# Two expert stages rearranged: whole-row weight loads, a new pair order and a split scatter in the first; permuted channels and two unsplit blocks in the second

## The chip, the cores and the metric

The kernel runs on one core of a Trainium2 chip. The metric is the device time of one execution in microseconds. Three runs of the kernel before took 1739.23, 1738.76 and 1736.85 us, median 1738.76 us.

## The reference

512 tokens of 1024 channels pass through two transformer blocks, everything in and out in float32. What matters here are the two mixture-of-experts parts:

```python
def expert_choice(h, w_router, w_gate, w_up, w_down):      # first block: 16 experts, FF 1024
    cap = CAP_FACTOR * l // N_EXPERTS                       # 64 tokens for each expert
    aff = softmax(h @ w_router)
    vals, idx = lax.top_k(swapaxes(aff, 1, 2), cap)
    xs = h[bidx, idx]
    hid = silu(xs @ w_gate) * (xs @ w_up)
    y = (hid @ w_down) * vals[..., None]
    return zeros_like(h).at[bidx, idx].add(y)
...
x = x + ga2 * expert_choice(hx2, ...)
...
def hierarchical_moe(h, ...):                               # second block: 16 experts, FF 256, top 2
    ...
    u = silu(h @ w_gate[e]) * (h @ w_up[e]) * combine[e]
    y = sum over e of u @ w_down[e]
```

The first block before that is an ada-norm, an mLSTM and a Fourier branch over the sequence and a context; the second has a conformer convolution, a forgetting attention and a cross attention ahead of its experts. A row norm ends each.

## The kernel before, in words

One class, `Builder`, writes the program in phases, and a scheduler orders the instructions of each engine by their place in the program and by due times. All weights that pass through the core come through one ring of 1-MB buffers, `raw` tiles of 128 partitions x 2048 float32. `self.raw` (L118 in its helper) lets SyncE issue the load of the next buffer in program order; a load waits for the readers of what the buffer held before. More buffers join the ring as memory comes free (`extra_raw`).

**First expert stage** (`phase_b`, from L1049). The 16 experts go in 8 pairs. 64 tokens of each of the two experts stand side by side in a tile of 128. One pair of them takes 24 MB of weights, 192 MB for the stage: `w_gate`, `w_up`, `w_down` of 1024x1024 float32 for each expert. A chunk of one load, `chunk_b`, is 512 rows by half of the columns (128x4x512), so a row of a load has 2 KB. For a pair:
- `gather` (L1069, its products L1077) picks the tokens by products of the residual `xres` with a 0/1 matrix `G`, 32 of 128x128x128 in float32. It stands inside the pair before.
- `pair_mm` (L1058) multiplies one half of the columns: gate half 0, up half 0, silu and product, four transposes (L1110), then the same of half 1, then down half 0 and half 1. The two experts' products (L1065, L1066) run beside each other in the two halves of the array's columns.
- After each down half, VectorE writes `y` = result times the gate vector `ga2` (L1117), TensorE multiplies it by a float32 matrix `PT` that holds the router's values at the tokens' places (L1120, 4 products), and VectorE adds the four tiles to the accumulator `acc` (L1122).

In the last pair the adds go to `xres`, from which the second block starts (L1222). Part of the first chunks are loaded ahead, in `phase_a2` (`keys`, `preload`).

**Second expert stage** (`phase_d`). For each expert up to 128 token rows are fetched from a memory copy of the normalised rows, `hmd`, which `write_rows` (L1643) fills; they are transposed (L1831) and split into a high and a low part in the reduced float format (`split`, L188 on ScalarE and L189 on VectorE). For each of 8 blocks of 128 channels the gate and up weights (128x512, `raw`) are split as well: `wH` on ScalarE (L129) and `wL` = raw - `wH` on VectorE (L130); three passes (L89, L90, L91) make one product. The weights are loaded in 1-KB rows. The down weights are split into `dH` (ScalarE) and `dL` (GpSimd, L1859), and the results are written to memory by an indirect transfer (L1883).

Of the kernel before, what the change touches and what calls it, by code (L numbers as in the profile page):

```python
# [8 lines left out]
F32 = mybir.dt.float32  # L9
F32R = mybir.dt.float32r  # L10
# [22 lines left out]
NRAW_B4 = 2  # L33
# [48 lines left out]
class Builder:  # L82
# [764 lines left out]
    def phase_a2(self, late, pb, right):  # L847
# [106 lines left out]
        keys = [(n, e, kk, h) for h in range(2) for n in ("w_gate_e", "w_up_e") for kk in (0, 4) for e in range(2)]  # L954
# [72 lines left out]
    def chunk_b(self, name, e, kk, half):  # L1027
        key = name, e, kk, half
# [15 lines left out]
    def phase_b(self, pb, right, G0):  # L1044
# [13 lines left out]
        def pair_mm(w, p, half, act):  # L1058
            ps = self.ps()
            for kk in (0, 4):  # L1060
                rA = chunk(w, 2 * p, kk, half)
                rB = chunk(w, 2 * p + 1, kk, half)
                for q in range(4):
                    k = kk + q
                    nc.tensor.matmul(ps[0:64, :], act[:, k, 0:64], rA[:, q, :], start=k == 0, stop=k == 7, tile_position=(0, 0))  # L1065
                    nc.tensor.matmul(ps[64:128, :], act[:, k, 64:128], rB[:, q, :], start=k == 0, stop=k == 7, tile_position=(0, 64))  # L1066
            return ps
# [16 lines left out]
        nxt = gather(0)  # L1084
        for p in range(8):
            xT = nxt
            if p == 0:
                nc.sync.dma_start(out=self.iota, in_=I["iota"])
                for e in range(2):
                    nc.sync.dma_start(out=ga2[:, e, :], in_=self.gad[1:2, e * 512:(e + 1) * 512].to_broadcast([128, 512]))  # L1090
            PT = xp.tile([128, 512], F32, tag="PT", name="PT", bufs=1)
            V.tensor_scalar(PT, self.iota, self.idxF[:, p:p + 1], self.valF[:, p:p + 1], op0=OP.is_equal, op1=OP.mult)
# [8 lines left out]
            hT = xp.tile([128, 8, 128], F32, tag="hidT", name="hidT", bufs=1)  # L1101
            for half in range(2):
                pg = pair_mm(w_g, p, half, xT)
                pu = pair_mm(w_u, p, half, xT)
# [7 lines left out]
                if half == 0 and p < 7:  # L1112
                    nxt = gather(p + 1)
# [925 lines left out]
```

## Time and profile before

| what | value |
|---|---|
| runs of the kernel before | 1736.85 to 1739.23 us, median 1738.76 us |
| the profiled execution: its own time | 1735.82 us |
| its span in the trace, granted clock over it | 1733.9 us, 0.975 |
| PE busy | 1580.3 us (91%) |
| PE weight loads | 1044.1 us (60%) |
| DVE, ACT, POOL busy | 881.7 (51%), 622.5 (36%), 536.7 (31%) us |
| moved by DMA | 381.22 MB, 220 GB/s on average |

The span is the time between the first and the last record of the profiled execution; 1.9 us of its own time lie around it. The shares are averages over stages that differ: the first expert stage takes the stretch from 544 to 1043 us, in which the DMA engines move about 386 GB/s, and the second expert stage the one from about 1520 to 1693 us, in which VectorE, ScalarE and TensorE are all busy. Both are read by windows, by the intervals between instructions that come once for each pair or expert, and by the waits.

### The profile page before, as it was taken

The numbers are of one execution on the slowest core, as the hardware profiler recorded it, in microseconds if no ns is written. First come the engines' busy times: TensorE is split into PE (matmuls) and PEld (weight loads), VectorE is DVE, ScalarE is ACT, GpSimd is POOL, SyncE is SP. The second block draws the span as 40 slices with busy tenths as digits, with TensorE's granted clock in tenths as the row PEclk, the third lists the DMA queues.
The fourth block names the chain that finished last, engine by engine and source line by source line (L and its number), as shares of the span: only waits on it lengthen the run. The fifth ranks groups of instructions, "written<-read, shape, count | busy, mean of one in ns | idle before, by whom it ended". The sixth has DMA issues, their size and how long they took to land. (4 is left out here: it accounts for less than half of the span.)

```text
span 1733.9 us, 20855 instructions
## 1 busy us (share of the span) xinstructions
PE 1580.3 (91%) x7734; PEld 1044.1 (60%) x7734; DVE 881.7 (51%) x1625; ACT 622.5 (36%) x1261; POOL 536.7 (31%) x433
## 2 busy tenths in 40 slices
PE   5988999999999999999999988999999988889984
PEld 3766677777776344344344326778666766666663
DVE  5388554433563212122122117998654464578886
ACT  3433354433432000000000015324763354478883
POOL 1213324334522000000000014575443342456654
PEclk9998999999999999999999998999999999899997
DMA  9533313445757999999999984323112329489934
GB/s 305 164 99 101 115 55 116 151 151 174 267 186 272 381 386 387 386 387 386 386 386 386 387 317 141 96 75 98 49 49 73 133 68 321 161 264 338 323 111 163
DMA packets 237227, 381.22 MB, mean 220 GB/s; under 512 B 16302, under 2 KB 107510, under 8 KB 237116
## 3 DMA queue, kind: packets, MB, share of 16 engines
q1 hardware_dynamic: 232796, 371.63, 61.2%
q0 software_dynamic: 4320, 8.16, 1.3%
q8 instruction: 63, 1.03, 0.3%
q14 instruction: 48, 0.39, 0.1%
HBM read 367.40 MB, written 19.93 MB: 223 GB/s over the span
## 5 line engine op out<-in xcount | busy, mean ns | idle before, releaser
L130 POOL TENSOR_TENSOR wL<-raw,wH 128x512 fp32r<-128x512 f32 x220 | 311.9, 1423 | 421.3 <-ACT wH L129 393.0
L129 ACT ACTIVATE wH<-raw 128x512 fp32r<-128x512 f32 x368 | 226.3, 629 | 283.8 <-PE ps L90 149.2
L1065 PE MATMUL ps<-raw,xT 128*64 128x512 f32 x512 | 228.5, 601 | 0.9 <-DMA raw<-in_w_up_e 0.9
L1066 PE MATMUL ps<-raw,xT 128*64 128x512 f32 x512 | 227.2, 601 | 1.6 <-DMA raw<-in_w_up_e 1.6
L1222 POOL TENSOR_TENSOR xg<-xres,raw 128x512 f32<-128x512 f32 x4 | 5.0, 1288 | 494.1 <-DVE xres L1122 494.1
L1066 PEld LDWEIGHTS ps<-raw,xT 128*64 128x64 f32 x512 | 69.3, 138 | 137.9 <-issue 132.2
L130 DVE TENSOR_TENSOR wL<-raw,wH 128x512 fp32r<-128x512 f32 x148 | 127.3, 906 | 27.0 <-ACT wH L129 25.5
L91 PE MATMUL ps<-raw,wL 128*128 128x512 f32 (+1 forms) x320 | 120.2, 376 | 2.9 <-POOL wL L130 2.9
L90 PE MATMUL ps<-raw,wH 128*128 128x512 f32 (+1 forms) x320 | 121.2, 379 | 0.0
L89 PE MATMUL ps<-raw,wH 128*128 128x512 f32 (+1 forms) x320 | 120.9, 379 | 0.0
L1107 DVE TENSOR_TENSOR hid<-hid,ps 128x512 f32<-128x512 f32 x16 | 11.0, 688 | 214.6 <-PE ps L1066 214.6
L1106 ACT ACTIVATE hid<-ps 128x512 f32<-128x512 f32 x16 | 9.6, 597 | 303.8 <-PE ps L1066 303.8
L1285 DVE SCALAR_TENSOR_TENSOR cacc<-upad,dwc,cacc 128x512 f32<-128x512 f32 x120 | 117.8, 1034 | 0.9
L1065 PE MATMUL ps<-raw,hidT 128*64 128x512 f32 x256 | 115.0, 596 | 0.0
L1066 PE MATMUL ps<-raw,hidT 128*64 128x512 f32 x256 | 113.5, 595 | 0.4 <-DMA raw<-in_w_down_e 0.4
L89 PE MATMUL ps<-hx,wH 128*128 128x512 f32 x224 | 91.7, 409 | 3.3 <-ACT wH L129 3.3
L91 PE MATMUL ps<-hx,wL 128*128 128x512 f32 x224 | 90.7, 405 | 2.2 <-POOL wL L130 2.0
L90 PE MATMUL ps<-hx,wH 128*128 128x512 f32 x224 | 90.4, 404 | 0.0
L1859 POOL TENSOR_TENSOR dL<-raw,dH 128x512 fp32r<-128x512 f32 x64 | 82.3, 1306 | 22.1 <-ACT dH L1858 21.6
L1066 PEld LDWEIGHTS ps<-raw,hidT 128*64 128x64 f32 x256 | 33.7, 137 | 72.1 <-issue 69.3
L1065 PEld LDWEIGHTS ps<-raw,xT 128*64 128x64 f32 x512 | 69.2, 138 | 11.0 <-issue 8.9
L1120 PE MATMUL pa<-y,PT 128*128 128x512 f32 x128 | 59.2, 605 | 12.3 <-DVE y L1117 12.3
(610 smaller groups left out, 3472.7 us busy)
## 6 DMA issues: line engine op xcount, KB each, us to landing
raw<-in_w_gate_e SPq DMA_DIRECT2D x64, 1024.0 KB
raw<-in_w_up_e SPq DMA_DIRECT2D x64, 1024.0 KB
raw<-in_w_down_e SPq DMA_DIRECT2D x64, 1024.0 KB
raw<-in_w_in SPq DMA_DIRECT2D x34, 1024.0 KB
raw<-in_w_ada SPq DMA_DIRECT2D x24, 1024.0 KB
raw<-in_expert_w_gate SPq DMA_DIRECT2D x32, 512.0 KB
raw<-in_expert_w_up SPq DMA_DIRECT2D x32, 512.0 KB
raw<-in_expert_w_down SPq DMA_DIRECT2D x16, 1024.0 KB
```

Of the source, the lines that this page charges most:

```text
L89: mm(ps, l[0], r[0], start=first, stop=False)
L90: mm(ps, l[0], r[1], start=False, stop=False)
L91: mm(ps, l[1], r[0], start=False, stop=last)
L129: i = self.nc.scalar.activation(out=H, in_=raw_ap, func=AF.Copy)
L130: j = (eng or self.lsub).tensor_tensor(out=L, in0=raw_ap, in1=H, op=OP.subtract)
L1065: nc.tensor.matmul(ps[0:64, :], act[:, k, 0:64], rA[:, q, :], start=k == 0, stop=k == 7, tile_position=(0, 0))
L1066: nc.tensor.matmul(ps[64:128, :], act[:, k, 64:128], rB[:, q, :], start=k == 0, stop=k == 7, tile_position=(0, 64))
L1106: AC.activation(out=hid, in_=pg, func=AF.Silu)
L1107: V.tensor_tensor(hid, hid, pu, op=OP.mult)
L1120: nc.tensor.matmul(ps, PT[:, t * 128:(t + 1) * 128], y, start=True, stop=True)
L1285: V.scalar_tensor_tensor(acc, src, c, acc, op0=OP.mult, op1=OP.add)
L1859: (nc.gpsimd, V)[DL[i]].tensor_tensor(out=L, in0=src, in1=H, op=OP.subtract)
```

## The change

In the first expert stage:
- A chunk is 256 whole rows (128x2x1024, rows of 4 KB in a load). A pair takes 8 chunks of gate, 8 of up, 8 of down, each a MB as before; only the last pair's down weights stay in half rows (`last_down`).
- `pair_mm` fills both halves of the columns at once, in two accumulators, so gate, up and down are each one run of 32 products.
- The gate products of pair p+1 are placed ahead of the down products of pair p.
- In the scatter the matrix is an exact 0/1 matrix in the reduced format, the router's value goes into `y` (L1122 of the new kernel), and `y` is split into `yH` (ScalarE) and `yL` (GpSimd, VectorE in the last pair). Two passes (`mm2`, L96 and L97) take the place of one float32 product.
- One extra raw buffer less (`NRAW_B4` 2 to 1): 16 buffers instead of 17.

In the second expert stage the rows of `hmd` are written with their channels permuted, so that a partition holds 8 channels that follow each other in the weights; a weight load of half an expert's gate or up is then one run of 4 KB for each partition. Blocks 3 and 7 of the 8 are multiplied in float32 from `raw` by an unsplit `xF`; six of eight are split as before.

```diff
-NRAW_B4 = 2
+NRAW_B4 = 1
...
-        return self.raw(self.I[name][0][e, kk * 128:(kk + 4) * 128, half * 512:(half + 1) * 512]
-                        .rearrange("(k p) c -> p k c", p=128), 4, 512)
+        return self.raw(self.I[name][0][e, kk * 256:(kk + 1) * 256, :].rearrange("(k p) c -> p k c", p=128), 2, 1024)
...
+        def pair_mm(w, p, act):
+            pss = [self.ps() for _ in range(2)]
+            for kk in range(4):
+                rs = [chunk(w, 2 * p + i, kk) for i in range(2)]
+                for q in range(2):
+                    k = 2 * kk + q
+                    for h, ps in enumerate(pss):
+                        for i, r in enumerate(rs):
+                            o = slice(64 * i, 64 * i + 64)
+                            nc.tensor.matmul(ps[o, :], act[:, k, o], r[:, q, h * 512:(h + 1) * 512], start=k == 0, stop=k == 7, tile_position=(0, 64 * i))
+            return pss
...
+        def scatter(p, py):
+            P = xp.tile([128, 512], F32R, tag="PT", name="PT", bufs=1)
+            V.tensor_scalar(P, self.iota, self.idxF[:, p:p + 1], None, op0=OP.is_equal)
+            for e in range(2):
+                y = xp.tile([128, 512], F32, tag="hid", name="y", bufs=3)
+                V.scalar_tensor_tensor(y, py[e], self.valF[:, p:p + 1], ga2[:, e, :], op0=OP.mult, op1=OP.mult)
+                H, L = (xp.tile([128, 512], F32R, tag="yS", name=x, bufs=3) for x in ("yH", "yL"))
+                AC.activation(out=H, in_=y, func=AF.Copy)
+                (nc.gpsimd if p < 7 else V).tensor_tensor(out=L, in0=y, in1=H, op=OP.subtract)
+                for t in range(4):
+                    ps = self.pa()
+                    self.mm2(ps, P[:, t * 128:(t + 1) * 128], (H, L), True, True)
...
+        pg = pair_mm(w_g, 0, xT)
         for p in range(8):
+            hid = silu(pg)
+            nxt = gather(p + 1) if p < 7 else None
+            hT = hidden(hid, pair_mm(w_u, p, xT))
...
+            else:
+                xT = nxt
+                pg = pair_mm(w_g, p + 1, xT)
+            scatter(p, pair_mm(w_d, p, hT) if p < 7 else last_down(hT))
...
-                    self.hm_last = nc.gpsimd.tensor_tensor(out=hs[e], in0=xres[:, t, c], in1=gm[:, c], op=OP.mult)
+                    x, g = (v.rearrange("p (q k) -> p k q", k=8)[:, 4 * e:4 * e + 4, :] for v in (xres[:, t, :], gm))
+                    self.hm_last = nc.gpsimd.tensor_tensor(out=hs[e].rearrange("p (k q) -> p k q", k=4), in0=x, in1=g, op=OP.mult)
...
-                r = self.raw_tile(4, 512)
+                r = self.raw_tile(2, 1024).rearrange("p i (k f) -> p i k f", k=4)
                 for i, w in enumerate((w_g, w_u)):
-                    nc.sync.dma_start(out=r[:, :, i * 256:(i + 1) * 256],
-                                      in_=w[e, kk * 128:(kk + 4) * 128, :].rearrange("(k p) f -> p k f", p=128))
+                    nc.sync.dma_start(out=r[:, i], in_=w[e].rearrange("(p k) f -> p k f", k=8)[:, kk:kk + 4, :])
...
+                nc.scalar.activation(out=xF[:, e2, :], in_=ps[:, 384:512], func=AF.Copy)
...
+                w, j = rs[k // 4][:, :, k % 4, :], 3 * (k // 4) + k % 4
+                if k % 4 == 3:
+                    nc.tensor.matmul(pgu, xF[:, k // 4, :], w, start=False, stop=k == 7)
+                    continue
```

On TensorE, in the first expert stage, this is a piece of one pair in the kernel before; `hid` transposed, then the row of tokens `bcI`, the gather and the scatter (`y`, `PT`) stand between products of single halves.

```order
L1110 MATMUL pa<-ident,hid 128x128 x4
L1038 MATMUL bcI<-ident,idxF 128x128
L1066 MATMUL ps<-raw,xT 64x512
L1065 MATMUL ps<-raw,xT 64x512
L1077 MATMUL pa<-G,xres 128x128 x32
...
L1066 MATMUL ps<-raw,hidT 64x512
L1065 MATMUL ps<-raw,xT 64x512
L1120 MATMUL pa<-y,PT 128x512 x4
L1066 MATMUL ps<-raw,xT 64x512
```

In the new kernel one pair reads on TensorE as follows, from the up products (`xT`, 6 and 25 of them, one more further up) over the gate products of the next pair (1 and 31) to its down products (`hidT`) and the scatter.

```order
L1068 MATMUL ps<-raw,xT 64x512 x6
L1079 MATMUL pa<-G,xres 128x128 x32
L1068 MATMUL ps<-raw,xT 64x512 x25
L1106 MATMUL pa<-ident,hid 128x128 x4
L1068 MATMUL ps<-raw,xT 64x512
L1106 MATMUL pa<-ident,hid 128x128 x4
L1068 MATMUL ps<-raw,xT 64x512 x31
L1068 MATMUL ps<-raw,hidT 64x512 x32
L96 MATMUL pa<-yH,PT 128x512 x3
L97 MATMUL pa<-yL,PT 128x512 x3
L96 MATMUL pa<-yH,PT 128x512
L97 MATMUL pa<-yL,PT 128x512
```

Both transposes now stand near the start of the next pair's gate products, and the scatter of both halves comes together behind the 32 down products, with a single product of the following up run between.

On SyncE's queue the loads of one pair stood like this before.

```order
L118 DMA raw<-in_w_down_e 128x4x512 x8
L118 DMA raw<-in_w_gate_e 128x4x512 x4
L118 DMA raw<-in_w_up_e 128x4x512 x4
L118 DMA raw<-in_w_gate_e 128x4x512 x4
L118 DMA raw<-in_w_up_e 128x4x512 x4
L118 DMA raw<-in_w_down_e 128x4x512 x8
```

In the new kernel they stand so, the last row being the last pair's down weights.

```order
L118 DMA raw<-in_w_gate_e 128x2x1024 x8
L118 DMA raw<-in_w_down_e 128x2x1024 x8
L118 DMA raw<-in_w_up_e 128x2x1024 x8
L118 DMA raw<-in_w_gate_e 128x2x1024 x8
...
L118 DMA raw<-in_w_down_e 128x4x512 x8
```

The number of loads is the same, 24 a pair; gate comes ahead of the previous pair's down, and the rows are twice as long.

On VectorE one expert of the second stage was this (a number behind a name tells the expert's tile apart).

```order
L1843 TENSOR_TENSOR hid_11205<-hid_11205,egu 128x256
L130 TENSOR_TENSOR wL<-raw,wH 128x512
L189 TENSOR_TENSOR xL_11209<-pa,xH_11208 128x512 x2
L1878 TENSOR_SCALAR y_11224<-py_11225,wslv 128x512
L189 TENSOR_TENSOR hidL<-pa,hidH 128x256
L130 TENSOR_TENSOR wL<-raw,wH 128x512 x7
```

It is now this.

```order
L1886 TENSOR_TENSOR hid_11176<-hid_11176,egu 128x256
L189 TENSOR_TENSOR xL_11180<-pa,xH_11179 128x384 x2
L1921 TENSOR_SCALAR y_11198<-py_11199,wslv 128x512
L189 TENSOR_TENSOR hidL<-pa,hidH 128x256
L1882 TENSOR_TENSOR wL<-raw,wH 128x512 x6
```

Two of the eight subtractions for the weights are gone, all six that are left stand in one run behind `hidL`, and the split of the rows is a quarter shorter.

## Rows read from the trace of the kernel before

**Rows 1.** Windows: PE, PEld, DVE, ACT, POOL busy (count); clock, DMA share, GB/s.

```profile
550.00:995.00 445.00, 420.23 (x2042) 178.84 (x2040) 89.74 (x175) 19.71 (x33) 0.00 (x0) 1.00 1.04 386
980.00:985.00 5.00, 5.00 (x22) 2.15 (x22) 0.00 (x0) 1.20 (x2) 0.00 (x0) 0.68 1.04 387
1000.00:1005.00 5.00, 5.00 (x26) 1.63 (x24) 0.00 (x0) 0.00 (x0) 0.00 (x0) 1.00 0.03 9
```

**Rows 2.** One line's TensorE products, 520 to 1060 us: min/median/max ns, first, last.

```profile
L1065 PE MATMUL ps<-raw,xT x512: 592/592/1061, 544.4 to 1016.0; 128*64 128x512 f32 x171
```

**Rows 3.** Timeline of DVE: start, duration, line, tiles, idle time before and its releaser.

```profile
662.97 0.69 DVE L1117 TENSOR_TENSOR y<-ps,ga 128x512 f32<-128x512 f32 x1 [6.32 <-PE ps L1065]
724.87 0.69 DVE L1117 TENSOR_TENSOR y<-ps,ga 128x512 f32<-128x512 f32 x1 [6.32 <-PE ps L1065]
1038.16 0.69 DVE L1117 TENSOR_TENSOR y<-ps,ga 128x512 f32<-128x512 f32 x1 [6.32 <-PE ps L1066]
```

**Rows 4.** Waits, 540 to 1040 us: total us, times, longest.

```profile
PE pa L1120 <- DVE y L1117: 12.3, 16, 0.8
PE ps L1066 <- DMA raw<-in_w_up_e: 1.6, 1, 1.6
```

**Rows 5.** Windows with transfers of other row lengths.

```profile
345.50:347.50 2.00, 2.00 (x18) 1.96 (x17) 0.95 (x2) 0.80 (x2) 1.04 (x1) 1.00 1.09 349
409.00:411.50 2.50, 2.50 (x12) 2.03 (x11) 0.00 (x1) 0.84 (x2) 1.30 (x2) 1.00 1.01 409
1697.00:1703.00 6.00, 5.47 (x22) 3.22 (x20) 3.69 (x5) 3.33 (x7) 6.00 (x5) 1.00 1.02 414
```

**Rows 6.** The loads in these windows, timeline of SyncE's queue.

```profile
342.18 0.37 SPq L118 DMA_DIRECT2D raw<-in_w_ada  x1
407.09 0.38 SPq L118 DMA_DIRECT2D raw<-in_mem  x1
1693.43 2.19 SPq L1919 DMA_DIRECT2D raw<-yd  x4
```

**Rows 7.** Timeline of PE in the first expert stage.

```profile
537.12 7.31 PE L1077 MATMUL pa<-G,xres 128*128 128x128 f32 x64
602.24 3.70 PE L1120 MATMUL pa<-y,PT 128*128 128x512 f32 x8 [0.78 <-DVE y L1117]
606.78 0.59 PE L1066 MATMUL ps<-raw,xT 128*64 128x512 f32 x1
607.21 0.59 PE L1066 MATMUL ps<-raw,xT 128*64 128x512 f32 x1
```

**Rows 8.** Timeline of PE, second expert stage.

```profile
1604.53 0.50 PE L90 MATMUL egu<-wL,xH 128*128 128x512 f32 x1 [1.14 <-DVE wL L130]
1615.67 0.50 PE L90 MATMUL egu<-wL,xH 128*128 128x512 f32 x1 [1.11 <-DVE wL L130]
1616.00 0.39 PE L91 MATMUL egu<-wH,xL 128*128 128x512 f32 x1
1616.23 0.40 PE L89 MATMUL egu<-wH,xH 128*128 128x512 f32 x1
```

**Rows 9.** Window of one expert, second expert stage.

```profile
1604.70:1615.80 11.10, 9.91 (x47) 7.57 (x48) 9.55 (x14) 9.10 (x17) 7.38 (x6) 1.00 0.92 303
```

**Rows 10.** A group, 1560 to 1694 us: count, busy us, mean ns, idle before.

```profile
L130 DVE TENSOR_TENSOR wL<-raw,wH 128x512 fp32r<-128x512 f32 x97 | 85.1, 933 | 1.1
```

**Rows 11.** Timelines of DVE and of POOL in one expert.

```profile
1611.67 6.35 DVE L130 TENSOR_TENSOR wL<-raw,wH 128x512 fp32r<-128x512 f32 x7
1607.14 0.69 DVE L130 TENSOR_TENSOR wL<-raw,wH 128x512 fp32r<-128x512 f32 x1
1613.76 1.29 POOL L1859 TENSOR_TENSOR dL<-raw,dH 128x512 fp32r<-128x512 f32 x1
```

**Rows 12.** Timeline of POOL ahead of the second expert stage.

```profile
1506.00 2.49 POOL L1643 TENSOR_TENSOR hm<-xres,raw 128x512 f32<-128x512 f32 x2
1516.57 1.24 POOL L1818 DMA_INDIRECT xsb<-hmd,trow  x1 [5.41 <-DVE s L1771]
```

More of the change, by code (lines that the diff above doesn't have):

```diff
@@ L953, in phase_a2 @@
         self.pre = {}
-        keys = [(n, e, kk, h) for h in range(2) for n in ("w_gate_e", "w_up_e") for kk in (0, 4) for e in range(2)]
+        keys = [(n, e, kk) for n in ("w_gate_e", "w_up_e") for kk in range(4) for e in range(2)]
         def preload(n):
@@ L1083, in phase_b, with last_down @@
             nc.sync.dma_start(out=rows2[8 * i:8 * i + 8], in_=n.rearrange("(k p) -> k p", p=128))
-        nxt = gather(0)
-        for p in range(8):
[L1086 to L1092, printed above, removed]
+        def last_down(act):
+            pss = [self.ps() for _ in range(2)]
+            for h, ps in enumerate(pss):
+                for kk in (0, 4):
+                    rs = [self.raw(I[w_d][0][14 + i, kk * 128:(kk + 4) * 128, h * 512:(h + 1) * 512].rearrange("(k p) c -> p k c", p=128), 4, 512)
+                          for i in range(2)]
+                    for k in range(kk, kk + 4):
+                        for i, r in enumerate(rs):
+                            o = slice(64 * i, 64 * i + 64)
+                            nc.tensor.matmul(ps[o, :], act[:, k, o], r[:, k - kk, :], start=k == 0, stop=k == 7, tile_position=(0, 64 * i))
+            return pss
@@ new lines, in hidden @@
+        def hidden(pg, pu):
+            hT = xp.tile([128, 8, 128], F32, tag="hidT", name="hidT", bufs=1)
+            for half in range(2):
+                V.tensor_tensor(pg[half], pg[half], pu[half], op=OP.mult)
+                ps = self.pa()
+                for q in range(4):
+                    nc.tensor.transpose(ps[:, q * 128:(q + 1) * 128], pg[half][:, q * 128:(q + 1) * 128], ident)
+                AC.activation(out=hT[:, 4 * half:4 * half + 4, :], in_=ps.rearrange("p (k s) -> p k s", k=4), func=AF.Copy)
+            return hT
@@ new lines, in silu @@
+        def silu(pg):
+            hid = [xp.tile([128, 512], F32, tag="hid", name="hid", bufs=3) for _ in range(2)]
+            for h in range(2):
+                AC.activation(out=hid[h], in_=pg[h], func=AF.Silu)
+            return hid
+        def scatter(p, py):
[8 more added lines that the diff above has]
+                for t in range(4):
+                    ps = self.pa()
+                    self.mm2(ps, P[:, t * 128:(t + 1) * 128], (H, L), True, True)
+                    c = slice(e * 512, (e + 1) * 512)
+                    V.tensor_tensor((acc if p < 7 else xres)[:, t, c], (acc if p else xres)[:, t, c], ps, op=OP.add)
@@ L1093, in phase_b @@
+        xT = gather(0)
+        nc.sync.dma_start(out=self.iota, in_=I["iota"])
+        for e in range(2):
+            nc.sync.dma_start(out=ga2[:, e, :], in_=self.gad[1:2, e * 512:(e + 1) * 512].to_broadcast([128, 512]))
+        pg = pair_mm(w_g, 0, xT)
+        for p in range(8):
+            hid = silu(pg)
+            nxt = gather(p + 1) if p < 7 else None
+            hT = hidden(hid, pair_mm(w_u, p, xT))
             if p == 7:
@@ L1823, in expert_in @@
         def expert_in(x):
[L1825 to L1826 removed]
+            xH = xp.tile([128, 6, 128], F32R, tag="xH", name="xH2", bufs=NXH)
+            xL = xp.tile([128, 6, 128], F32R, tag="xL", name="xL2", bufs=NXH)
+            xF = xp.tile([128, 2, 128], F32, tag="xF", name="xF2", bufs=NXH)
             for e2 in range(2):
```

53 lines of the change are left out of this document (11 added, 42 removed).

## The prediction

> **What bounds the kernel now.** I read the windows first, because the change touches two stages and the averages over the span mix them. In the first expert stage TensorE is busy 420 of 445 us while the DMA engines are fully busy at 386 GB/s [rows 1]: two limits lie close together, and the reader has to find out which ends last. The interval between two scatters of the same kind tells TensorE's pace: y at 662.97 and at 724.87, so 61.9 us for a pair [rows 3]. The transfers' pace follows from their size: a pair takes 24 loads of 1.0486 MB, 25.17 MB, and at 386 GB/s that is 65.2 us. So the transfers are slower by 3.3 us a pair, but TensorE began at 544.4 [rows 2] with a full ring of 17 buffers, and a lead of 17 loads (46 us) lasts almost to the end. The waits agree: TensorE waited 1.6 us for a weight, once, and 12.3 us for `y` [rows 4]. The stage is balanced: whoever shortens only one side gains next to nothing.
>
> In the second expert stage the window of one expert has TensorE at 9.91, VectorE at 9.55, ScalarE at 9.10 of 11.10 us and the transfers at 0.92 [rows 9]; an expert takes 11.14 us (1604.53 to 1615.67), and both rows show TensorE idle 1.1 us until VectorE's `wL` [rows 8]. VectorE is not full, but its seven subtractions behind `hidL` take 6.35 us in a row [rows 11], and TensorE is at their end.
>
> **First expert stage, TensorE.** The expert products stay: a product of one expert shows as two records 0.43 us apart, with the other expert's beside it [rows 7], so 48 steps a pair (gate, up, down, each 8 blocks by 2 halves) take 48 x 0.86 = 41.3 us, before and after. The gather stays: 7.2 us for the first one, from 537.12 to the first product at 544.4 [rows 2, 7]. The scatter changes. Before, twice a pair, eight records in 3.70 us and a wait for `y` [rows 7], near 4.7 with the pipeline's restart, so 9 to 10 us. After, 4 tiles by 2 halves by 2 passes: a reduced-format pass of the same width follows the one ahead by 0.23 us (1616.00 to 1616.23) [rows 8], 16 x 0.23 = 3.7 us. The wait comes on top: `y` 0.69 us, `yH` about as much, then `yL` on POOL 1.29 (as for `dL`) [rows 3, 11], of which the passes that need `yH` alone cover 0.7; some 2 us, and the second half waits for nothing. That makes 5.7. The saving is 3.3 to 4.5 us, and the transposes of the hidden values, now behind a gate product, may give 0.8 more. TensorE's pair comes to 61.9 - 5.4 at best and 61.9 - 3.3 at worst, 56.5 to 58.6. The new work on ScalarE and POOL is free: POOL did nothing in the stage and ScalarE 19.7 of 445 us [rows 1].
>
> **First expert stage, transfers.** What decides is whether 4-KB rows move faster than 2-KB rows. Before does not show it on these weights; the nearest rows are loads of the same kind. Rows of 1 KB (`w_ada`) gave 349 GB/s, the 2-KB rows here 386, rows of 4 KB 409 (`in_mem`) and 414 (`yd`), with all engines full each time [rows 1, 5, 6]. The ends are 386 (no gain) and 414. I take 409, the load from an input by the same queue. A load then lasts 2.564 us instead of 2.716.
>
> The Trainium skill ("DMA: Bandwidth & Descriptors", section "Why small descriptors are slow") has a fixed overhead of about 3 cycles a packet, beside a cycle for each 32 bytes; by that, 4-KB packets are 2.2% faster than 2-KB ones, 395 GB/s, the last y falls at 1020.8 and the stage gains 17 us. The rows go against so small an effect, 6% between 386 and 409, and the measurement decides. The same page's section "Where 436 GB/s comes from" lets the memory side bind at about 358 GB/s, by which row length could not matter at all; 386 over 445 us contradicts the figure.
>
> The ring has 16 buffers now. All are full when TensorE starts, the first pair of loads is used up by 547.8 and the transfers run again from about 549.7. 176 of 192 loads are left: 168 x 2.564 + 8 x 2.716 (the last down, still 2 KB) = 452.5 us, until 1002.2; the products on the last load take 3.4, and the last y stands at 1005.5 instead of 1038.2 [rows 3]: 32.7 us earlier. TensorE by itself would end at 544.4 + 8P - 11 (the first gather lies ahead, 7.2, and the last scatter behind, 3.8): for P = 56.5 at 985, for 58.6 at 1002. So the transfers end last up to P = 59.1, and the shorter scatter matters only because it keeps TensorE under this. Against the gain stands a hole like the one before, where the queue moved 9 GB/s from 1000 to 1005 [rows 1] because `gg` had taken a slot of the ring; with TensorE now the one who waits, buffers are free earlier, and I deduct 2.5 us (0 to 5). Gain 30 us; by the ends of the rate, 7 to 38. Removing the 17th buffer costs its lead of one load, 2.6 us, which is in this count. The new order (gate ahead of the previous down) leaves the number of loads alone and only shifts which one TensorE waits for.
>
> **Second expert stage.** Without its waits TensorE needs for an expert 24 passes x 0.23, eight transposes 0.8, twelve down passes 2.8, two transposes 0.1, restarts 0.2, about 9.4 us. Six passes go (-1.4), two float32 products of 0.86 come (+1.7), with two changes of format about 0.1: 9.85. VectorE loses two of eight subtractions (933 ns on average, 0.69 undisturbed) [rows 10, 11] and a quarter of `xL`: 9.55 - 1.5 = 8.1. ScalarE loses two `wH`, gains two small `xF`: 9.1 becomes 8.2. So TensorE becomes the limit if the subtractions come in time: the fifth of the run is wanted about 8.0 us after the last product of the expert before, and comes at about 7.5 (hidden values, `hidL`, then five by 0.65, one of them stretched beside POOL's subtraction, which ran at 1613.76 while VectorE's seven took 6.35 instead of 7 x 0.62 = 4.3 us) [rows 11]. A cover of 0.5 us is thin. If it holds, 11.14 - 9.85 = 1.29 an expert, and over 14 experts in steady state (16 less the first and last) 18; I take 16.4, since the traces of experts differ by some tenths. If it fails the period is 10.95 and the gain 2.5. Transfers need 3.15 MB an expert, 7.7 us at 409 beside 0.92 of 11.1 us so far with 1-KB and 4-KB rows mixed [rows 9]; faster rows make this smaller.
>
> The permuted write of `hmd` reads both operands with a step of 32 bytes on POOL. Before, two take 2.49 us [rows 12]; the trace has no such read. The ends are no change and twice the time, 5 us for the last two. POOL then waits 5.4 us for the routing before its first row fetch [rows 12], and the cover is spoilt only beyond about 4 us, where the fill of `xsb`, queued behind it, and the fetch come later; at nothing. The Trainium skill ("GPSIMD Engine Reference", "Performance pitfalls for Q7 kernels") gives +50% for such a step; by it the last two take 3.7 us, inside the cover.
>
> **Sum.** 1735.8 (the profiled execution's own time) - 30 - 16.4 = 1689.4. The median of the runs is 2.9 above that execution, so 1692 for the median.
>
> **Rivals.**
> 1. Row length does nothing: 386 stays. Last y 549.7 + 176 x 2.716 + 3.4 = 1031.2, gain 7; 1735.8 - 7 - 16.4 + 2.9 = 1715. For it: 386 is flat over the whole stage. Against: two 4-KB loads above 409 [rows 5]. 10%.
> 2. VectorE still ends last in the second stage, period 10.95: 1735.8 - 30 - 2.5 + 2.9 = 1706. For it: the thin cover, and the stretched subtractions [rows 10]. Against: two of eight are gone. 22%.
> 3. TensorE stays the limit in the first stage, because `y` to `yL` runs over three engines while nothing is left to cover it: P = 61 gives a last y at 1021.4, gain 16.8, total 1705. For it: the wait for `y` now stands behind both halves at once. Against: it would have to cost 7 us where I count 2. 12%.
> 4. Slower: TensorE, which now waits for weights in every pair, is granted its lower level. In this stage the clock was 1.00 except for stretches like 980 to 985, 0.68 between the two levels of 1.2 and 2.4 GHz, with TensorE busy throughout [rows 1]. If the clock averages c in the stage, a pair takes 56.5/c and the last y stands at 544.4 + 8 x 56.5/c - 11. The second stage's 16.4 us are used up at a last y of 1054.6, P = 65.2, c = 0.87; at 0.80 the time is 1735.8 + 60 - 16.4 + 2.9 = 1782. Against it: one short drop in 445 us. 4%.
>
> **How the numbers follow.** Forecast 50%, with a range of its own of 1684 to 1700 (rate 414 at the one end, TensorE near 58 or a gap at the other); rivals as given, 2% for what I don't see. 1692 is the likeliest. For eight in ten: below 1676 would need more than both gains at their best; above 1720 lies rival 4 and rivals 1 and 2 together. Runs spread by 0.14%, so 0.2% (3.5 us) is what can be told from no change. All but rival 4 are faster: 0.93 faster, 0.03 the same (several rivals at once), 0.04 slower.
>
> **What the new profile would show.** Right: 405 to 415 GB/s over the first expert stage; TensorE's waits there name the weights' transfers, not `y`; y's 61 to 62 us apart once the ring's lead is gone, 56 to 59 before; the last y near 1006; an expert of the second stage in 9.8 to 10.1 us, with hardly a wait for `wL`; `hm` longer and no later first fetch. Wrong: 386 to 395 GB/s (rivals 1); periods of 11 with waits for `wL` (2); waits for `yL` or `y` of 5 us a pair with the transfers idle in between (3); a clock below 0.9 over tens of us (4).

## The result and the profile after

The changed kernel takes 1712.94 us (median of four runs, 1708.35 to 1715.06), the kernel before 1738.99 us beside it. The ratio is 0.985 with a 95% interval of 0.982 to 0.987: 22 to 31 us faster, where 47 was forecast. The profiled execution took 1714.9 us, its span is 1713.1 us, the granted clock 0.969. The sign held, and the time lies between the 1676 and 1720 that were given for eight in ten, but outside the forecast's own range of 1684 to 1700; the size was a little over half. The time is nearest to that of rival 1 (1715), whose mechanism did not come: the rate below shows it. So the total alone would have pointed at the wrong cause.

The way to see where it went is to cut both traces at the same five marks and compare the lengths (all from the timelines of the two kernels: the first product of the first pair, the last `y`, the first residual add ahead of `hm`, the first fetch of expert rows, the last indirect store).

| stretch (us) | before | after | gain | forecast |
|---|---|---|---|---|
| start to the first product of pair 0 | 544.4 | 546.2 | -1.8 | 0 |
| first product to last `y` | 493.8 | 472.5 | 21.3 | 30 |
| last `y` to the residual add | 445.8 | 446.2 | -0.4 | 0 |
| residual add to the first fetch of rows | 32.6 | 39.3 | -6.7 | 0 |
| first fetch to the last store | 173.8 | 166.6 | 7.2 | 16.4 |
| last store to the end | 43.5 | 42.3 | 1.2 | 0 |

The rows add up to 20.8 us, the difference of the two profiled executions; that of the kernel before lies under all four of its runs, that of the changed kernel is one of its two longest, and the medians differ by 26. The start is left unexplained: in the experiments below it lies between 542.1 and 547.8 without an edit ahead of it. The two expert stages gave 29 us instead of 46, and 6.7 were lost between them. The rest of this section shows the lines for each; the lines of before that they answer to are named.

**First expert stage.** Windows, columns as in [rows 1]:

```profile
800.00:900.00 100.00, 97.78 (x473) 41.24 (x474) 16.27 (x35) 4.62 (x8) 2.56 (x2) 1.00 1.03 409
995.00:1000.00 5.00, 5.00 (x19) 2.92 (x19) 0.00 (x0) 1.19 (x2) 0.00 (x0) 0.50 0.62 230
1000.00:1010.00 10.00, 9.01 (x38) 2.83 (x36) 0.00 (x0) 0.00 (x0) 0.00 (x0) 0.97 0.64 222
```

The rate is 409 GB/s, the value taken, instead of 386; and near the end there is a hole, with 230 GB/s from 995 to 1000 and less behind. VectorE's timeline gives the pairs ([rows 3]; here both halves of a pair come together):

```profile
669.28 1.54 DVE L1122 SCALAR_TENSOR_TENSOR y<-ps,valF,ga 128x512 f32<-128x512 f32 x2 [28.29 <-PE ps L1068]
727.48 1.54 DVE L1122 SCALAR_TENSOR_TENSOR y<-ps,valF,ga 128x512 f32<-128x512 f32 x2 [28.30 <-PE ps L1068]
907.62 1.54 DVE L1122 SCALAR_TENSOR_TENSOR y<-ps,valF,ga 128x512 f32<-128x512 f32 x2 [31.50 <-PE ps L1068]
969.02 1.54 DVE L1122 SCALAR_TENSOR_TENSOR y<-ps,valF,ga 128x512 f32<-128x512 f32 x2 [31.53 <-PE ps L1068]
1018.76 0.75 DVE L1122 SCALAR_TENSOR_TENSOR y<-ps,valF,ga 128x512 f32<-128x512 f32 x1 [0.48 <-PE ps L1096]
```

A pair takes 58.2 us while the ring still has a lead (669.28 to 727.48) and 61.4 us when it is gone (907.62 to 969.02; 24 loads at 409 GB/s take 61.5): TensorE's pace first, the transfers' pace afterwards, both as forecast. But the last `y` comes 49.7 us after that of the pair before. On TensorE's timeline, in this last stretch:

```profile
961.00 4.48 PE L1068 MATMUL ps<-raw,hidT 128*64 128x512 f32 x16 [0.48 <-DMA raw<-in_w_down_e]
966.12 3.65 PE L1068 MATMUL ps<-raw,hidT 128*64 128x512 f32 x12 [0.64 <-DMA raw<-in_w_down_e]
970.48 0.97 PE L96 MATMUL pa<-yH,PT 128*128 128x512 f32 x3 [0.72 <-ACT yH L1124]
...
991.84 5.38 PE L1148 MATMUL pa<-rows,ident 16*128 16x128 f32 x32
997.15 9.68 PE L1096 MATMUL ps<-raw,hidT 128*64 128x512 f32 x34
1007.82 3.78 PE L1096 MATMUL ps<-raw,hidT 128*64 128x512 f32 x16 [0.99 <-DMA raw<-in_w_down_e]
```

Until 968 TensorE waits for weights; after that only once, for 0.99 us, at the load that came out of the hole. Scatter, 32 up products, `gg` (L1148) and 32 down products are TensorE's own work, and a piece of it ran at the lower of the clock's two levels (0.50 from 995 to 1000, from the small products of `gg` on). SyncE's queue shows the hole itself, a load waiting from about 988 to 1002.6:

```profile
985.98 2.56 SPq L118 DMA_DIRECT2D raw<-in_w_down_e  x1
1002.57 1.47 SPq L118 DMA_DIRECT2D raw<-in_w_down_e  x3
```

**Between the stages.** POOL and VectorE, timelines ([rows 12] has the same stretch of before):

```profile
1470.96 4.07 POOL L1675 TENSOR_TENSOR hm<-xres,raw 128x512 f32<-128x512 f32 x2 [1.93 <-DVE xres L1217]
1474.98 0.55 POOL L235 TENSOR_TENSOR rr<-rv,mhalf 128x1 f32<-128x1 f32 x1
1490.80 4.07 POOL L1675 TENSOR_TENSOR hm<-xres,raw 128x512 f32<-128x512 f32 x2
1504.22 1.24 POOL L1850 DMA_INDIRECT xsb<-hmd,trow  x1 [6.68 <-DVE s L1791]
```

```profile
1477.54 2.00 DVE L230 TENSOR_TENSOR rv<-ss 128x1 f32<-128x1 f32 x1 [1.74 <-ACT nsq L1226]
```

Two `hm` take 4.07 us instead of 2.49. The last two are hidden, as forecast: POOL still idles 6.68 us before the first fetch. But `rr`, which the routing needs, stands behind the first ones in POOL's queue, and VectorE's tiny `rv` is longer beside them: the first two of the four take 1.36 and 2.00 us, in the kernel before 0.59 and 0.25.

**Second expert stage.** One expert's window, and ScalarE and TensorE in it ([rows 8, 9]):

```profile
1579.57:1590.20 10.63, 9.99 (x45) 7.32 (x44) 8.22 (x12) 8.02 (x18) 7.73 (x7) 1.00 0.94 361
```

```profile
1578.89 0.93 ACT L188 ACTIVATE xH<-pa 128x384 fp32r<-128x384 f32 x2
1581.50 0.28 ACT L1867 ACTIVATE xF<-pa 128x128 f32<-128x128 f32 x1 [1.68 <-DVE xL L189]
1581.67 0.62 ACT L1901 ACTIVATE dH<-raw 128x512 fp32r<-128x512 f32 x1
1584.48 0.39 ACT L188 ACTIVATE hidH<-pa 128x256 fp32r<-128x256 f32 x1
```

```profile
1576.14 0.50 PE L90 MATMUL egu<-wL,xH 128*128 128x512 f32 x1 [0.62 <-DVE wL L1882]
1586.77 0.50 PE L90 MATMUL egu<-wL,xH 128*128 128x512 f32 x1 [0.64 <-DVE wL L1882]
```

An expert takes 10.63 us. VectorE and ScalarE have nearly the busy times that the prediction gave them (8.22 and 8.02 against 8.1 and 8.2), yet TensorE still waits for `wL`. What is new is ScalarE's 1.68 us in front of `xF`: it idles until VectorE has made `xL` out of the same PSUM tile `pa`, into which TensorE transposed the rows. `dH` and `hidH` are queued behind `xF`, and VectorE's `hidL` and run of `wL` wait for `hidH`, so all of them start later.

### The profile page after: what moved, and what is told of

Read it like the earlier page. It is cut to its first block, busy times and chain, and to the rows that moved or that the text cites. A ratio compares the mean times of both kernels' runs of the same rounds, so it can differ in the third digit from the quotient of the medians.

```text
span 1713.1 us, 20867 instructions
## 1 busy us (share of the span) xinstructions
PE 1579.9 (92%) x7702; PEld 1049.7 (61%) x7702; DVE 856.2 (50%) x1595; ACT 613.5 (36%) x1277; POOL 564.9 (33%) x447
## 5 line engine op out<-in xcount | busy, mean ns | idle before, releaser
L129 ACT ACTIVATE wH<-raw 128x512 fp32r<-128x512 f32 x240 | 149.6, 628 | 256.8 <-PE ps L90 149.7
L1068 PE MATMUL ps<-raw,xT 128*64 128x512 f32 x1024 | 240.8, 595 | 0.0
L1068 PEld LDWEIGHTS ps<-raw,xT 128*64 128x64 f32 x1024 | 74.3, 137 | 137.3 <-issue 133.4
L1125 POOL TENSOR_TENSOR yL<-y,yH 128x512 fp32r<-128x512 f32 x14 | 17.9, 1278 | 419.4 <-ACT yH L1124 409.2
L1122 DVE SCALAR_TENSOR_TENSOR y<-ps,valF,ga 128x512 f32<-128x512 f32 x16 | 12.0, 751 | 228.0 <-PE ps L1068 206.8
L1068 PE MATMUL ps<-raw,hidT 128*64 128x512 f32 x448 | 109.3, 594 | 2.8 <-DMA raw<-in_w_down_e 2.8
L1882 DVE TENSOR_TENSOR wL<-raw,wH 128x512 fp32r<-128x512 f32 x96 | 88.4, 976 | 4.6 <-ACT wH L1881 3.3
L1124 ACT ACTIVATE yH<-y 128x512 fp32r<-128x512 f32 x16 | 10.0, 626 | 212.7 <-DVE y L1122 212.7
L91 PEld LDWEIGHTS ps<-raw,wL 128*128 128x128 f32 x320 | 61.2, 191 | 15.0 <-POOL wL L130 3.4
L89 PEld LDWEIGHTS ps<-raw,wH 128*128 128x128 f32 x320 | 61.4, 192 | 12.2 <-ACT raw L188 1.1
L90 PEld LDWEIGHTS ps<-raw,wH 128*128 128x128 f32 x320 | 61.1, 191 | 11.4 <-issue 0.5
```

The costliest lines, as they stand in the source:

```text
L89: mm(ps, l[0], r[0], start=first, stop=False)
L90: mm(ps, l[0], r[1], start=False, stop=False)
L91: mm(ps, l[1], r[0], start=False, stop=last)
L129: i = self.nc.scalar.activation(out=H, in_=raw_ap, func=AF.Copy)
L1068: nc.tensor.matmul(ps[o, :], act[:, k, o], r[:, q, h * 512:(h + 1) * 512], start=k == 0, stop=k == 7, tile_position=(0, 64 * i))
L1125: (nc.gpsimd if p < 7 else V).tensor_tensor(out=L, in0=y, in1=H, op=OP.subtract)
```

## The experiments

Three theories, one for each loss. **First stage:** the ring loses a buffer to `gg` and stalls, and TensorE's own work ends last. **Between:** `hm` with a step delays `rr` and `rv`. **Second stage:** `xF` behind `xL`. Each has a rival in its expectation. The stretches quoted are those of the table above, from one profiled execution each; where an edit doesn't touch them they lie from 470.5 to 472.5 us in the first stage, from 166.6 to 167.5 in the second, and from 444.2 to 448.6 between the last `y` and the residual add.

**Half rows again** (`e4_half`): the chunks of before in the new order.

```diff
...
+            for kk in (0, 4):
+                rs = [[chunk(w, 2 * p + i, kk, h) for i in range(2)] for h in range(2)]
...
```

> The changed kernel, but the chunks of the first expert stage are half rows again (512 rows by 512 columns, 2 KB a row), in the new order of the work. Theory: the row length alone sets the rate: 386 GB/s instead of 409, 0.15 us more a load, over some 160 loads 24 us; the last y comes near 1041 and the time is about 1735. Rival: the order and the shorter scatter made the gain and row length does little: the rate is 386 but TensorE's own path ends last, so the time stays within 8 us of the changed kernel's 1713.

1741.89 us, ratio 1.003 (1.002 to 1.005) to the kernel before: slower than it. First product to last `y` takes 494.9 us.

```profile
800.00:900.00 100.00, 89.53 (x448) 41.04 (x446) 21.67 (x46) 5.36 (x9) 3.85 (x3) 0.98 1.05 386
```

The rate is 386 again and TensorE now idles a tenth of the time. The whole gain of the first stage hangs on the row length; the new order and the scatter alone give nothing, since the transfers bound them. What whole rows would give in the old order wasn't tried. The theory stands for the stage (the last `y` at 1041.1 where 1041 was expected), but the time is 7 us above the 1735 expected and 5.5 above the kernel before: the stretch behind the last `y` is 451.0 us instead of 446.2. Both halves of the last pair end together there, and eight adds stand in a row behind them, which accounts for 1.3 us; the rest is not explained.

**The old scatter in the new order** (`e8_f32scatter`): one float32 product with the value in the matrix.

```diff
...
-                    self.mm2(ps, P[:, t * 128:(t + 1) * 128], (H, L), True, True)
+                    nc.tensor.matmul(ps, P[:, t * 128:(t + 1) * 128], y, start=True, stop=True)
...
```

> The changed kernel, but the scatter of the first expert stage is one float32 product again with the router's value in the matrix, in the new order and with whole-row loads. Theory: the two-pass scatter is what keeps TensorE under the transfers' pace: with 16 float32 records twice a pair (6.9 us) in place of 3.7, less the wait for yH and yL (about 2 us), TensorE's pair goes from 58.2 to 59.5 to 61.5 us in the first pairs, the last y comes 4 to 10 us later and the time is 1717 to 1723. Rival: the transfers bound the pairs anyway (61.4 us in the last three), so the last y moves by under 3 us.

1713.5 us, ratio 0.987 (0.986 to 0.989), overlapping that of the changed kernel; first product to last `y` 471.1 us, no longer than 472.5.

```profile
667.73 0.69 DVE L1122 TENSOR_TENSOR y<-ps,ga 128x512 f32<-128x512 f32 x1 [28.23 <-PE ps L1068]
727.08 0.69 DVE L1122 TENSOR_TENSOR y<-ps,ga 128x512 f32<-128x512 f32 x1 [28.23 <-PE ps L1068]
```

A pair takes 59.35 us against 58.2. The theory of this run fell: what the two passes save, the longer chain over ScalarE and POOL gives back, all but 1.2 us a pair, and the transfers hide that. So 2.5 of the 3.7 us by which TensorE's pair fell from 61.9 are due to the rest of the new order; which part of it wasn't taken apart.

**The slot of `gg`** in three forms. `e1b_ring` only takes an entry out of the ring when `gg` is made:

```diff
             if p == 7:
+                i = self.nraw % len(self.raws)
+                self.raws, self.nraw = self.raws[i:] + self.raws[:i], 0
+                self.raws.remove(self.rawp)
                 gg = self.gg = self.rawp.tile([128, 2, 1024], F32, tag="raw", name="raw")
```

> The changed kernel with nothing but one rawp entry taken out of the ring when gg is made, gg staying where it is. Theory: the hole in the queue before the last loads goes, but TensorE's own work behind the last pair's loads is what ends last, so the last y comes 1 to 3 us earlier only (1016 to 1018) and the time falls by 1 to 3 us. Rival: the hole is the cause of the late end and with it gone the last y comes before 1010.

`e1_gg` does that and moves the whole block ahead of the last pair's up products:

> The changed kernel, but the tile gg is made at the start of the last pair, ahead of its up products, and one of the ring's three rawp entries is taken out of the ring for it, so that no load is sent to a buffer that was given away. Theory: the queue's hole from 986 to 1002.6 us in the changed kernel is a load of the last down weights that was given the buffer of the first of them, because gg had taken a slot of the ring; without it the last loads are issued by about 992, the last y comes at about 1006 instead of 1018.8, TensorE then being the limit of the last pair (up ends near 990, then 14 us of down products), and the time falls by 10 to 13 us, to 1700 to 1703. Rival: TensorE is late anyway and the hole hides behind it: the last y moves by under 3 us. Second rival: the ring, now 15 buffers, starves TensorE and the gain is lost again.

`t1_tail` moves it one pair further up and puts the last pair's up products ahead of the down products of the pair before:

```diff
...
+        hid = silu(pg)
+        pu = pair_mm(w_u, 7, xT)
+        py = pair_mm(w_d, 6, hT)
+        hT = hidden(hid, pu)
+        scatter(6, py)
+        scatter(7, last_down(hT))
...
```

> The changed kernel with another end of the first expert stage: gg is made at the start of the pair before the last with one rawp entry of the ring taken out for it, and the last pair's up products (and their loads) stand ahead of the down products of the pair before. Theory: in the changed kernel TensorE ends last because behind the last load of the down weights of the pair before (y at 970) it still has 46 us of work (scatter, gg, 32 up and 32 down products, waits) against 41 us of transfers; with only down products behind it, the last y follows the last load by some 3.5 us and comes at about 1008 to 1010 instead of 1018.8, so the time falls by 9 to 11 us, to 1702 to 1704. Rival: the transfers end at 1010 or later whatever TensorE does, so the last y comes no earlier than 1015 and the gain is under 4 us, as with gg alone (1.5 to 2.3).

| kernel | median | ratio to before | first product to last `y` |
|---|---|---|---|
| changed | 1712.94 | 0.9847 (0.982 to 0.987) | 472.5 |
| `e1b_ring` | 1710.23 | 0.9842 (0.983 to 0.986) | 469.0 |
| `e1_gg` | 1710.38 | 0.9847 (0.983 to 0.987) | 468.7 |
| `t1_tail` | 1707.09 | 0.9834 (0.982 to 0.985) | 468.3 |

The whole times can't be told apart from the changed kernel; the stretch is 3.5 to 4.2 us shorter in all three, and the queue has no hole any more. In `e1b_ring` VectorE's timeline reads:

```profile
966.05 1.54 DVE L1122 SCALAR_TENSOR_TENSOR y<-ps,valF,ga 128x512 f32<-128x512 f32 x2 [31.55 <-PE ps L1068]
1012.55 0.75 DVE L1122 SCALAR_TENSOR_TENSOR y<-ps,valF,ga 128x512 f32<-128x512 f32 x1 [0.29 <-PE ps L1096]
```

Without the hole it is still 46.5 us from the `y` of the last pair but one to the last `y`, and none of TensorE's waits there names a transfer: TensorE's own work sets the end. But not all of the 3.5 us is the hole's. The granted clock behind `gg` differs from one execution to the next, also where nothing in this stage was edited (windows of the changed kernel and of `e2_xf`, whose edit lies in the second stage; the clock is the third number from the end):

```profile
985.00:1005.00 20.00, 19.78 (x93) 10.26 (x91) 1.38 (x2) 3.58 (x6) 0.00 (x0) 0.83 0.74 262
985.00:1005.00 20.00, 18.91 (x94) 8.98 (x92) 1.38 (x2) 3.58 (x6) 0.00 (x0) 0.91 0.83 301
```

| kernel | hole | granted clock, 985 to 1005 | first product to last `y` |
|---|---|---|---|
| changed | yes | 0.83 | 472.5 |
| `e3_hm` | yes | 0.83 | 472.3 |
| `e2_xf` | yes | 0.91 | 470.6 |
| `e6_split8` | yes | 0.91 | 470.5 |
| `c5_small` (edit of `e1b_ring`) | no | 0.83 | 470.7 |
| `e1b_ring` | no | 0.91 | 469.0 |

At the same clock the hole cost 1.5 to 1.8 us, and the longer stay at the lower level 1.7 to 2.0. `e1b_ring` did what was expected of it. The gains of 10 us that I gave `e1_gg` and `t1_tail` didn't come: in `t1_tail`, too, no wait of TensorE names a transfer from 906 on, and at the same mean clock (0.83, in its case from 910 to 930) it is only 2.4 us shorter than `c5_small`.

**`hm` unpermuted** (`e3_hm`): POOL multiplies as before, the channels are picked at the transposes.

```diff
...
-                    nc.tensor.transpose(ps[:, q * 128:(q + 1) * 128], x[:, k * 128:(k + 1) * 128], ident)
+                    nc.tensor.transpose(ps[:, q * 128:(q + 1) * 128], x.rearrange("p (q k) -> p k q", k=8)[:, k, :], ident)
```

> The changed kernel, but hm is written unpermuted, as before the change, and the channels are picked with a step at the transposes, in TensorE's weight load. Theory: POOL's 4.07 us for a pair of hm instead of 2.58 delays rr, which stands behind it on POOL, and VectorE's rv beside it, for each of four token tiles; without it the first fetch of rows comes 5 to 7 us earlier against the last residual add, and the time falls by as much, unless the transposes get longer (0.8 us an expert now; at twice that, 13 us would be lost and the time would rise by 6). Rival: the stretch is longer because TensorE's clock was granted lower there (0.77 against 0.83): then hm is short again and the first fetch comes no earlier.

1707.95 us, ratio 0.984 (0.982 to 0.985). The residual add to the first fetch takes 34.0 us instead of 39.3, the second stage 166.8, unchanged.

```profile
1474.47 1.29 POOL L1675 TENSOR_TENSOR hm<-xres,raw 128x512 f32<-128x512 f32 x1
1500.32 1.24 POOL L1850 DMA_INDIRECT xsb<-hmd,trow  x1 [6.66 <-DVE s L1791]
```

The step costs POOL 0.75 us for each `hm` (4.07 us for two, against 1.29 for one), and TensorE's weight load nothing. `rv` is back at 0.59 and 0.25 us. 5.3 of the 6.7 us are shown to be `hm`'s. For the other 1.4 the traces name a candidate: here and in the changed kernel four subtractions `wL` of the second stage (0.68 us each) stand among the routing's steps on VectorE, and in the kernel before, in `c3_one` (32.5 us to the first fetch) and in `e6_split8` (37.9 us, with the stepped `hm`) none does. No run changed that alone.

**`xF` first** (`e2_xf`): one line moved.

```diff
+                nc.scalar.activation(out=xF[:, e2, :], in_=ps[:, 384:512], func=AF.Copy)
                 b = slice(3 * e2, 3 * e2 + 3)
                 self.split(ps[:, 0:384].rearrange("p (k s) -> p k s", k=3), (xH[:, b, :], xL[:, b, :]))
-                nc.scalar.activation(out=xF[:, e2, :], in_=ps[:, 384:512], func=AF.Copy)
```

> The changed kernel, but the copy to xF stands ahead of the split of the same PSUM tile instead of behind it. Theory: in the changed kernel ScalarE waits 1.68 us an expert for VectorE's xL before it may read the same PSUM tile for xF; its dH copies, hidH and by them VectorE's hidL and wL run come 1.3 us later, and TensorE's 0.64 us wait for wL is their end. With xF first the period of an expert falls from 10.63 to 9.8 to 10.0 us, the wait for wL nearly goes, and the time falls by 8 to 11 us. Rival: VectorE's subtractions beside POOL's set the period: it stays at 10.4 to 10.6, gain under 3 us.

1702.46 us, ratio 0.981 (0.979 to 0.983); first fetch to last store 155.8 us instead of 166.6. ScalarE no longer waits for VectorE between the copies, and TensorE is never idle:

```profile
1573.45 0.28 ACT L1865 ACTIVATE xF<-pa 128x128 f32<-128x128 f32 x1
1573.62 0.49 ACT L188 ACTIVATE xH<-pa 128x384 fp32r<-128x384 f32 x1
1573.99 0.28 ACT L1865 ACTIVATE xF<-pa 128x128 f32<-128x128 f32 x1
```

```profile
1560.00:1600.00 40.00, 40.00 (x182) 30.36 (x181) 33.30 (x47) 33.55 (x70) 31.53 (x25) 1.00 0.99 376
```

From one `hidL` to the next (1568.41 to 1578.15) an expert takes 9.74 us. The wait of 1.68 us cost 10.8 us in the stage; the rival (VectorE beside POOL) is out.

**All eight blocks split, long runs kept** (`e6_split8`).

> The changed kernel, but all eight blocks of the second stage are split as before the change; the permuted channels, the 4-KB runs of the loads and the late store of hm stay. Theory: the loads were never what this stage waited for, so without the two float32 blocks an expert takes the 11.1 us of the kernel before again, and the time rises by 14 x 0.5 = 7 us against the changed kernel, to about 1720. Rival: the longer rows had made this stage faster: an expert takes 10.6 to 10.8 us and the time stays within 3 us of 1713.

1718.47 us, ratio 0.990 (0.989 to 0.992); the second stage takes 174.6 us, as before the change (173.8), an expert 11.12 us:

```profile
1600.37 0.50 PE L90 MATMUL egu<-wL,xH 128*128 128x512 f32 x1 [1.11 <-DVE wL L1877]
1611.49 0.50 PE L90 MATMUL egu<-wL,xH 128*128 128x512 f32 x1 [1.10 <-DVE wL L1877]
```

While VectorE's subtractions end last, the 4-KB runs are worth nothing in this stage, and the two unsplit blocks are worth all of the gain. Whether 1-KB rows would hold the stage back at `e2_xf`'s 9.74 us an expert, where the DMA engines are 0.99 busy, wasn't tried.

**Versions.** `c2_all` joins `t1_tail`, `e2_xf` and `e3_hm`; `c3_one` also splits block 3 again, so that one block is unsplit; `c4_late` is `c2_all` with the scatter's products emitted behind the next pair's up products; `c5_small` joins the three small edits `e1b_ring`, `e2_xf`, `e3_hm`.

> The changed kernel with the three mends together: the end of the first stage as in t1_tail, the copy to xF ahead of the split, hm unpermuted with the step in the transposes' weight load. Theory: the three lie one after the other in time and add up: 9 to 11, 11 and 5 us, so 1713 becomes 1686 to 1689, the time forecast for the change itself. Rival: what is saved early is given back later, at the first fetch of the second expert stage or in the tail: above 1695.

> As c2_all, but only block 7 is multiplied in float32 and seven are split. Theory: TensorE is the limit of an expert with xF first (9.74 us without a wait); three passes of 0.23 us for a float32 product of 0.86 save 0.17 us an expert, 2.7 us in all, if VectorE, which gets one more subtraction of 0.65 to 1.0 us on 8.4 of 9.74, still keeps up. Rival: it doesn't, an expert takes 10.0 us or more and the time is 4 us or more above c2_all.

> As c2_all, with the products of a pair's scatter emitted behind the next pair's up products (in the last pair between the two halves of the down products), while y, yH and yL are made right after the down products. Theory: TensorE waits some 3 us a pair for y, yH and yL and is the limit of the first pairs and of the end of the stage; with other products to do meanwhile its pair falls from 58.2 to 55 to 56, the last y comes 3 to 6 us earlier than in c2_all and the time is 1687 to 1690 against 1693. Rival: the transfers, which bound the middle, take the gain: within 2 us of c2_all.

> The changed kernel with three small edits: one rawp entry out of the ring when gg is made (as e1b_ring), the copy to xF ahead of the split (as e2_xf), hm unpermuted with the step in the transposes' weight load (as e3_hm). Theory: the stretches follow one another, so the gains add: from the first product to the last y 469 us (-3.5), from the residual to the first fetch 34.0 (-5.3), the second expert stage 157 (-10): the time is 19 us under the changed kernel's, 1691 to 1695, the same as c2_all without its other order at the end. Rival: the order at the end was worth something more, and the time is 3 us or more above c2_all's 1693.

| kernel | median | ratio to before | first stage | to the first fetch | second stage |
|---|---|---|---|---|---|
| `c2_all` | 1692.85 | 0.975 (0.973 to 0.976) | 468.5 | 34.0 | 157.0 |
| `c3_one` | 1710.06 | 0.986 (0.985 to 0.988) | 468.2 | 32.5 | 173.8 |
| `c4_late` | 1725.32 | 0.994 (0.992 to 0.995) | 501.9 | 34.0 | 156.7 |
| `c5_small` | 1693.28 | 0.976 (0.975 to 0.977) | 470.7 | 33.9 | 156.9 |

`c2_all` and `c5_small` agree: the gains add, and the other order at the end is worth nothing that can be told in the times. By their ratios both lie 0.9 to 1% under the changed kernel; `c2_all` stayed above the 1686 to 1689 expected for it by the gain that `t1_tail` didn't bring.

`c3_one` fell by the rival's mechanism, and further. With seven subtractions VectorE is late again, and the full wait of before is back at a period of 11.15 us:

```profile
1576.94 0.51 PE L90 MATMUL egu<-wL,xH 128*128 128x512 f32 x1 [1.09 <-DVE wL L1893]
1588.10 0.50 PE L90 MATMUL egu<-wL,xH 128*128 128x512 f32 x1 [1.11 <-DVE wL L1893]
```

The 0.17 us less of TensorE's work that it was made for turned into 1.4 us more.

`c4_late` fell altogether. The scheduler spread the gather and the scatter in small groups among the expert products, and a pair takes 65.6 us. TensorE's timeline of one such piece:

```profile
708.23 1.60 PE L1079 MATMUL pa<-G,xres 128*128 128x128 f32 x12
709.77 3.65 PE L1068 MATMUL ps<-raw,xT 128*64 128x512 f32 x12
713.34 1.60 PE L1079 MATMUL pa<-G,xres 128*128 128x128 f32 x12
714.88 1.93 PE L1068 MATMUL ps<-raw,xT 128*64 128x512 f32 x4
```

Six expert products (two records each) take 3.57 us from their start to the next group's. In a long run 32 take 13.95 us, 0.436 each, so six would be 2.6. The starts of the single records tell why: in a long run two records, one of each expert, start together every 0.43 us, but in the group of twelve only the first eight do (709.77, 710.25, 710.68, 711.11); the last four start alone (711.53 to 712.82), and so do the four of the next group, which take 1.93 us. The groups cut the run so that the experts' products no longer stand side by side, and TensorE shows as busy all the while. Counted over a pair, `c4_late` has 80 steps with two records and 32 with one (747.7 to 813.3), the changed kernel 92 and 8 (669.28 to 727.48), the kernel before 96 and none. The 12 more steps against the changed kernel are 5.2 of the 7.4 us that the pair grew by; the rest is open.

## Why the prediction came out as it did

Right were the mechanism of the first stage (row length sets the rate: 409 taken, 409 measured, and 386 when the length is undone) and TensorE's work for an expert (9.85 given, 9.74 once nothing makes it wait). TensorE's pair came out in its range (56.5 to 58.6 given, 58.2 measured), but partly by luck, since its parts were wrong: the scatter saved 1.2 us and not 3.3 to 4.5, the expert products did not stay as they were (100 steps of 0.43 us instead of 96, 1.7 us more), and the rest of the new order gave what was missing. Rivals 1 and 4 are out: the rate rose, and the clock stayed at 1.00 through the pairs, apart from stretches such as 995 to 1000 (0.50, the lower level, from the small products of `gg` on). Rival 3 is out for most of the stage, where the transfers bounded the late pairs. One of the signs fell all the same: TensorE waited 8.3 us for `yH` and `yL` in the stage and 3.8 for weights. Rival 2 came half true: VectorE's `wL` ends last again, at 10.63 us an expert, but because it starts late and not because its run is too long. Three terms of the sum were wrong.

**"The transfers end last up to P = 59.1".** (The bound itself is 59.0 by the prediction's own terms.) The end was put at the later of two sums, each along one resource to the end: the transfers' at 1005.5, TensorE's at 999 for P = 58.2. The right sum switches: transfers up to the last down weights of the pair before (TensorE was through with them at 969), then TensorE's own work from there, 46.5 us in `e1b_ring`, against 16 x 2.564 = 41 us for the loads still to come. That ends at 1015.5. On top came the hole, 1.5 to 1.8 us (2.5 had been set aside for it), and in this execution 1.7 to 2.0 us more at the lower clock, for which the sum had no term: 1018.8. 21.3 us instead of 30.

**"ScalarE loses two `wH`, gains two small `xF`".** The copy was counted by its duration, and its wait at nothing. Here a third reader of a PSUM tile, placed behind another engine's read, added a wait; placed ahead of it, in `e2_xf`, it added none. 1.68 us of waiting on ScalarE, which has the least work of the three engines, moved `hidH` and the run of subtractions and ate the cover of 0.5 us that the text called thin. 7.2 us instead of 16.4, and `e2_xf` gives the missing part back. The Trainium skill ("PSUM — Partial Sum Buffer", section "PSUM bank collisions raise a hardware error") says that ScalarE and VectorE must not read the same quadrant of one bank at the same time, and that the compiler's scheduler puts a dependency between two such instructions; the wait of 1.68 us in the trace agrees. I had not weighed that rule.

**"The cover is spoilt only beyond about 4 us".** The bounds of the price were right (2.04 us against 1.29 for one `hm`, between no change and twice), but the cover was looked up behind the last pair only. Ahead of the others nothing was free: `rr` follows them on POOL, and the routing follows `rr`. 6.7 us lost, 5.3 of them shown. The Trainium skill ("GPSIMD Engine Reference", "Performance pitfalls for Q7 kernels") gives +50% for kernels that read with a step of more than 8 bytes; this case measured +58% for POOL's multiply (1.29 to 2.04).

The wrong saving of the scatter cost the forecast nothing, since the transfers hid it.

## What to carry to other kernels

When two resources are nearly balanced, the end of a stage is not the later of the two totals: cut it at the last point where one made the other wait and add what each still has to do behind that point. An instruction that is cheap in time but shares a tile, a bank or a queue is priced by what waits behind it, and the place to look is the engine that isn't the bottleneck. Before a few us between two executions are put down to an edit, the clock that each was granted in that stretch has to be compared. An operation that is hidden where it runs last may still sit on the path where it runs first: look up the cover of each instance.

## What the runs showed of the hardware that was not expected

- Sustained loads in rows of 2 KB moved 386 GB/s, in rows of 4 KB 409, over hundreds of us and at full engines in both (`e4_half` against the changed kernel). That is 6%; the smaller effect that the prediction weighed beside it was 2.2%, 395 GB/s.
- On TensorE, a finer mixture of products cost the pairing of two experts in the array's columns: in a long run two records start every 0.43 us, but of twelve in a group that the order had cut off, four started alone (3.57 us instead of 2.6), and so did the four of the next group (1.93 us), with the engine shown as busy throughout (`c4_late`).
- Behind the same small products of `gg`, kernels with the same first stage were granted a mean clock of 0.91 or of 0.83 from 985 to 1005, and the stage was 1.7 to 2.0 us longer with the lower one.
- A weight load for a transpose with a step of 32 bytes between elements costs nothing that can be seen (166.8 against 166.6 us for the stage; with `xF` first, where TensorE never waits, 9.76 us an expert against 9.74), while the same step costs POOL's multiply 58%.
- VectorE's `rv` on a single column took 1.36 and 2.00 us beside POOL's stepped multiply, and 0.59 and 0.25 us beside the unstepped one, in the kernel before and again in `e3_hm`.
